# A hybrid decoder block: the attention stretch in source order on every engine, and a PSUM bank of its own for the scans' unused operand

## The chip, the cores and the metric

The kernel runs on one core of a Trainium2 chip. The core has TensorE (PE in the profile; its weight loads are PEld), VectorE (DVE), ScalarE (ACT), GpSimd (POOL) and SyncE (SP), which issues the transfers. The metric is the device time of one execution in microseconds (us), the median of the runs shown.

## The reference

One decoder layer over 2048 tokens of 1024 columns. Three token mixers run on one normalised input projection, their outputs are normalised per head, joined, projected by `w_out` and added to the input; a SwiGLU feed-forward follows. The change touches the stretch in which the mixers run. The attention there is stick-breaking attention with 6 heads of 64 columns:

```python
z = einsum('bhqd,bhkd->bhqk', q, k) * d ** -0.5         # strictly causal
A[t, s] = sigmoid(z[t, s]) * prod_{s < j < t} (1 - sigmoid(z[t, j]))
out = A @ v
```

The other two mixers (4 heads each) are gated linear recurrences over the tokens:

```python
S_t = diag(f_t) S_{t-1} + k_t^T v_t ;  o_t = q_t S_t
```

## The kernel before, in words

The program is traced from top to bottom; a planner then orders the instructions of each engine. It keeps data dependences, prefers what stands earlier in the source, and puts a later instruction ahead where its own costs say that an earlier one isn't ready. The order so made is fixed: at run time each engine works through its list and waits where an operand isn't there.

Three phases follow one another: the input projections (to about 753 us), the attention stretch (753 to about 1615 us), and the output projection's rest with the feed-forward.

**The attention stretch.** It is cut into 240 slots (line 1301 and the loop after it). A unit is one head, one group of 512 queries and one block of 512 keys; each unit has four slots, one for 128 queries each. In a slot `n` the source calls, in this order:

- `z_step(n)`: TensorE writes the scores `z` into one of two PSUM banks (pool `f_pz`). ScalarE makes `kp = sigmoid(-z)` (L994) and a second sigmoid of `z` (L997), which goes into the SBUF tile `w`, or back into `z` for those slots whose weights VectorE multiplies (`on_dve`: slot 0 of a unit, or slots 0 and 2 in the first query group; 66 of 240). VectorE's scan (L998) makes the running products `pr` out of `kp`; its second tensor operand takes no part in the result (`op1=ALU.bypass`) and is a broadcast column of `z`. Then `w = w * pr` (or `z * pr`) on VectorE (L1002) or on GpSimd (L1004). There are two `kp` tiles, two `pr` tiles and 7 `w` buffers.
- half of the slot's share of recurrence steps (`rec_step`). Such a step has TensorE write chunk scores `sch` or `scg` into a bank of the pool `c_pss` (three banks), VectorE read them out under a mask (L1082, `st_h`, `st_g`) and multiply the queries by decays (L1078, L1119), and GpSimd multiply keys and decays (L1113, L1124, L1128). Outputs, transposed keys and updates of the state go through the same three banks.
- `t_step(n - 5)`: TensorE transposes four 128-column pieces of `w` into `wt` (L107), ScalarE copies them to `wth` (L1014, 8 buffers).
- the rest of the recurrence steps, or, when the recurrences are done, one step of the output projection (`out_.steps()`: the products `po`, norms on VectorE, L830 to L862).
- `a_step(n - 7)`: TensorE multiplies `wth` with the values.

TensorE's instructions of this stretch go through the class `Chain`, which ties each to the one before it without a semaphore, so that TensorE runs them in source order:

```python
for n in (self.last, self.after):
    if n is not None:
        tc.add_manual_dep(i, n, NOSYNC, reason="order")
```

The other engines' orders are the planner's. The transfers of SyncE are the planner's too, and the change doesn't touch that.

Of the kernel before, what the change touches and what calls it, by code (L numbers as in the profile page):

```python
# [8 lines left out]
F32 = mybir.dt.float32  # L9
# [4 lines left out]
AF = mybir.ActivationFunctionType  # L14
ALU = mybir.AluOpType
AX = mybir.AxisListType
PSUM = bass.MemoryType.PSUM
DRAM = bass.MemoryType.DRAM

P = 128  # L20
# [7 lines left out]
LAG_T = 5  # L28
# [34 lines left out]
def hybrid_block(ctx: ExitStack, tc: tile.TileContext, x, norm_mix_g, w_in, gla_w_decay,  # L63
# [2 lines left out]
    nc = tc.nc  # L66
    x, out = x[0], out[0]
    w_in, w_out, w_up, w_dn = w_in[0], w_out[0], w_ffn_up[0], w_ffn_down[0]
    act, dve, pool, pe, dma = nc.scalar, nc.vector, nc.gpsimd, nc.tensor, nc.sync


    def rsqrt_newton(small, v, n, tag):
# [19 lines left out]
    class Chain:  # L92
# [13 lines left out]
        def transpose(self, *a, **k):  # L106
            self._add(nc.tensor.transpose(*a, **k))  # L107

    tpe = [pe]
    NOSYNC = mybir.DependencyInfo(mybir.DependencyClass.NoSync,  # L110
                                  mybir.DependencyReason.SCHED_ONLY)

    def mm3(ps, pairs, n_lo=None):

        n = len(pairs)
# [8 lines left out]
    def open_pool(stack, name, bufs, space=None, side=None):  # L124
        kw = {} if space is None else {"space": space}
        if side is not None:
            kw["side"] = side
        return stack.enter_context(tc.tile_pool(name=name, bufs=bufs, reuse_waits="tile", **kw))
# [206 lines left out]
    class Stage:  # L335


        def __init__(self, p, stg, xtp, half):
            self.p, self.half, self.xtp = p, half, xtp
            self.b = [stg.tile([P, KH, 512], F32, tag=f"sg{j}", name=f"stg{p}_{j}")  # L340
                      for j in range(4)]
            self.xs = {}
# [585 lines left out]
    with ExitStack() as ph:  # L928
# [8 lines left out]
        prc = ExitStack()  # L937
        rio = open_pool(prc, "c_io", NB)
        rec = open_pool(prc, "c_rec", 2)
        ps_s = open_pool(prc, "c_pss", 3, PSUM)  # L940
        ps_o = ps_s
        tpe[0] = ch

# [10 lines left out]
        for g in G_ORDER:  # L954
            for h in range(0, SH, 2):
                for c in range(g, -1, -1):
                    for j in range(2):
                        u = Unit()
                        u.h, u.g, u.c, u.diag, u.i, u.j = h + j, g, c, c == g, len(units), j
                        units.append(u)  # L960

        def z_step(u, b):
            h, g, c = u.h, u.g, u.c
            if b == 0:
                if u.diag:
                    u.q = sio.tile([P, 2, 512], F32, tag="sq", name=f"sq{h}_{g}", bufs=3)
                    for s in range(2):
                        dma.dma_start(u.q[64 * s:64 * s + 64],
                                      sq_s[h // 2][g][:, 64 * (h % 2):64 * (h % 2) + 64, :]
                                      .rearrange("j p t -> p j t"))  # L970
                    u.carry = [1.0] * 4
                else:
                    p = units[u.i - 2]
                    u.q, u.carry = p.q, p.last
                u.last = []
                k = sio.tile([P, 512], F32, tag="sk", name=f"sk{h}_{g}_{c}")
                dma.dma_start(k, sk_s[h][c].rearrange("j p t -> (j p) t"))
                if u.j == 0:
                    u.v = sio.tile([P, 4, P], F32, tag="sv", name=f"sv{h}_{g}_{c}")
                    dma.dma_start(u.v, sv_s[c][:, h * SD:(h + 2) * SD]  # L980
                                  .rearrange("(n p) d -> p n d", p=P))
                u.k, u.ws = k.bitcast(F32R), []
            n = (b + 1) * P if u.diag else 512
            q = u.q.bitcast(F32R)[:, :, b * P:(b + 1) * P]
            z = ps_z.tile([P, 512], F32, tag="z", name=f"z{h}_{g}_{c}_{b}")[:, :n]
            ch.matmul(z, q[:, 0], u.k[:, :n], start=True, stop=False)
            ch.matmul(z, q[:, 1], u.k[:, :n], start=False, stop=not u.diag)
            if u.diag:
                ch.matmul(z[:, b * P:], identb, negm, start=False, stop=True)
            kp = kps[b % NKP][:, 512 - n:]  # L990
            w = sbw.tile([P, 512], F32, tag="w", name=f"w{h}_{g}_{c}_{b}", bufs=7)[:, :n]
            at = 4 * (g - c) + 2 * u.j + b // 2
            pr = prs[b % 2][:, at:at + 513]
            act.activation(kp[:, :n], z, AF.Sigmoid, scale=-1.0)  # L994
            kr = kp[:, n::-1] if n < 512 else kp[:, ::-1]
            on_dve = b in DVE_B0 if g == 0 else b == DVE_B
            act.activation(z if on_dve else w, z, AF.Sigmoid)  # L997
            dve.tensor_tensor_scan(pr[:, n::-1], kr, z[:, 0:1].to_broadcast([P, n + 1]),  # L998
                                   u.carry[b], op0=ALU.mult, op1=ALU.bypass)
            u.last.append(pr[:, 0:1])  # L1000
            if on_dve:
                dve.tensor_tensor(w, z, pr[:, 1:n + 1], op=ALU.mult)  # L1002
            else:
                pool.tensor_tensor(w, w, pr[:, 1:n + 1], op=ALU.mult)  # L1004
            u.ws.append(w)

        def t_step(u, s):
            t0 = s * P if u.diag else 0
            nm = f"{u.h}_{u.g}_{u.c}_{s}"
            wt = ps_w.tile([P, 512], F32, tag="wt", name="wt" + nm)  # L1010
            for b in range(t0 // P, 4):
                ch.transpose(wt[:, b * P:(b + 1) * P], u.ws[b][:, s * P:(s + 1) * P], ident)
            wh = sbw.tile([P, 512], F32, tag="wth", name="wth" + nm, bufs=8)[:, t0:]
            act.activation(wh, wt[:, t0:], AF.Copy)  # L1014
            u.wt = getattr(u, "wt", []) + [(wh, t0)]

# [275 lines left out]
        def rec_step(part):  # L1292
            nonlocal ns
            while ns < REC_STEPS * ((done + part) / total) ** REC_POW:
                ns += 1
                if next(step, 0) == 0:
                    return 1
            return 0

        outs = None  # L1300
        for n in range(n_slot + LAG_A):
            d = 0.0
            if n < n_slot:
                z_step(units[n // 4], n % 4)
                d = (n % 4 + 1) / 16 if units[n // 4].diag else 0.25
            if outs is None and rec_step(d / 2):
                for _ in wo_step:
                    pass
                prc.close()
                out_.open()  # L1310
                outs = out_.steps()
            if 0 <= n - LAG_T < n_slot:
                t_step(units[(n - LAG_T) // 4], (n - LAG_T) % 4)
            if outs is None:
                rec_step(d)
            else:
                for _ in range(OUT_RATE):
                    out_done = next(outs)
            done += d
            if folds:  # L1320
                o_step(*folds.pop())
            if 0 <= n - LAG_A < n_slot:
                a_step(units[(n - LAG_A) // 4], (n - LAG_A) % 4)
            if n >= WO_SLOT and n % 4 == 0:
                next(wo_step, None)
        o_step(*folds.pop())
# [289 lines left out]
```

## Time and profile before

| | |
|---|---|
| time, median of 3 runs | 3163.24 us (3161.28 to 3166.27) |
| profiled execution | 3166.77 us, span 3164.4 us |
| mean granted TensorE clock | 0.947 of full speed |
| PE busy over the span | 2836.1 us (90%) |
| DVE | 2115.8 us (67%) |
| ACT | 1282.6 us (41%) |
| POOL | 1423.3 us (45%) |

The first scan of line 998 starts at 754.9 us and the last at 1601.0 us; the last recurrence product of line 1078 starts at 1405.0 us. A busy time is the sum of an engine's instruction times; a wait is idle time of an engine, put down to what released it. An engine whose share is high in a stretch can still be waiting for another in that stretch, so the waits are read next to the shares.

### The profile page before, as it was taken

How to read it: one execution, taken by the hardware profiler on the slowest of the kernel's cores; microseconds unless marked ns; L12 is line 12 of the kernel's file. 1: busy time of each engine (PE TensorE's matmuls, PEld its weight loads, DVE VectorE, ACT ScalarE, POOL GpSimd, SP SyncE). 2: the span in 40 equal slices, each digit the busy share in tenths (PEclk: the TensorE clock that was granted, in tenths of full speed). 3: DMA queues.
4: the chain of work that ended last, by engine and by line, in shares of the span. 5: the costliest groups of instructions: out<-in, count | busy, mean ns of one | idle time of the engine just before them, and what ended most of it. 6: DMA issues, size and time to landing. Idle time of an engine off the chain costs nothing.

```text
span 3164.4 us, 43263 instructions
## 1 busy us (share of the span) xinstructions
PE 2836.1 (90%) x14882; PEld 2321.6 (73%) x14882; DVE 2115.8 (67%) x3808; ACT 1282.6 (41%) x2386; POOL 1423.3 (45%) x1402
## 2 busy tenths in 40 slices
PE   5898999997888888888788799999999998999887
PEld 5887878987666666665556578888788887777766
DVE  8886665876778777888867565555755553574453
ACT  5554534453555554554532243333433332322222
POOL 5342444344655555542221244444544443566244
PEclk8999999998989988998988899999999999999998
DMA  3534442436533322223345442222422224832474
GB/s 121 154 106 139 133 137 94 128 94 170 164 104 99 93 82 80 76 96 95 101 144 190 139 137 89 81 80 80 147 80 85 87 89 163 325 120 80 136 259 150
DMA packets 346091, 389.78 MB, mean 123 GB/s; under 512 B 59152, under 2 KB 258064, under 8 KB 344080
## 3 DMA queue, kind: packets, MB, share of 16 engines
q1 hardware_dynamic: 341776, 381.77, 38.1%
q0 software_dynamic: 4096, 5.25, 0.5%
q8 instruction: 118, 1.93, 0.3%
q14 instruction: 101, 0.83, 0.1%
HBM read 278.93 MB, written 108.00 MB: 122 GB/s over the span
## 4 chain that ended last, share of the span: by engine, by line
PE 56%; DVE 16%; DMA 5%; issue 5%; POOL 2%; ACT 2%; SPq 1%; DVEq 0%; POOLq 0%; ACTq 0%
PE gu L1404 9%; PE gu L1405 9%; PE gu L1403 8%; PE dn L1569 4%; DVE pr L998 4%; PE dn L1570 4%; PE dn L1571 3%; PE z L104 3%; PE av L104 2%; PE sch L104 2%; PE wt L107 2%; DVE m L840 1%; PE po L104 1%; PE scg L104 1%; DVE hq L1078 1%
## 5 line engine op out<-in xcount | busy, mean ns | idle before, releaser
L1404 PE MATMUL gu<-al,uh 128*128 128x512 f32 x1232 | 482.7, 392 | 7.0 <-DVE al L249 6.8
L1403 PE MATMUL gu<-ah,uh 128*128 128x512 f32 x1232 | 481.7, 391 | 5.0 <-ACT ah L248 4.9
L1405 PE MATMUL gu<-ah,ul 128*128 128x512 f32 x1232 | 481.0, 390 | 0.0
L249 POOL TENSOR_TENSOR ul<-bs,uh 128x512 fp32r<-128x512 f32 x176 | 241.3, 1372 | 240.8 <-ACT uh L248 236.5
L1004 POOL TENSOR_TENSOR w<-w,pr 128x512 f32<-128x512 f32 (+1 forms) x174 | 194.6, 1119 | 279.3 <-DVE pr L998 208.5
L1569 PE MATMUL dn<-dbh,dah 128*128 128x512 f32 x616 | 232.5, 407 | 52.3 <-ACT dbh L248 38.9
L1404 PEld LDWEIGHTS gu<-al,uh 128*128 128x128 f32 x1232 | 232.2, 188 | 61.5 <-DVE al L249 13.5
L249 POOL TENSOR_TENSOR ul<-us,uh 128x512 fp32r<-128x512 f32 x132 | 177.1, 1342 | 214.3 <-ACT uh L248 214.3
L1403 PEld LDWEIGHTS gu<-ah,uh 128*128 128x128 f32 x1232 | 232.5, 189 | 55.2 <-ACT ah L248 7.1
L1405 PEld LDWEIGHTS gu<-ah,ul 128*128 128x128 f32 x1232 | 232.3, 189 | 47.8
L245 DVE TENSOR_TENSOR h<-h,gu 128x512 f32<-128x512 f32 x176 | 120.9, 687 | 204.9 <-PE gu L1405 123.0
L104 PE MATMUL z<-sk,sq 128*128 128x512 f32 (+1 forms) x480 | 175.8, 451 | 86.8 <-DVE pr L998 46.0
L1570 PE MATMUL dn<-dbl,dah 128*128 128x512 f32 x616 | 242.9, 397 | 7.9 <-POOL dbl L249 7.8
L1571 PE MATMUL dn<-dbh,dal 128*128 128x512 f32 x616 | 240.0, 394 | 0.0
L248 ACT ACTIVATE uh<-bs 128x512 fp32r<-128x512 f32 x176 | 111.3, 634 | 305.1 <-PE gu L1404 300.8
L994 ACT ACTIVATE kp<-z 128x512 f32<-128x512 f32 (+1 forms) x240 | 128.1, 534 | 258.7 <-PE z L104 233.7
L104 PEld LDWEIGHTS z<-sk,sq 128*128 128x128 f32 x480 | 82.6, 213 | 180.5 <-DVE pr L998 73.3
L998 DVE TENSOR_TENSOR_SCAN pr<-kp,pr,z 128x513 f32<-128x513 f32 x144 | 182.1, 1271 | 20.4 <-ACT w L997 12.6
L1569 PEld LDWEIGHTS dn<-dbh,dah 128*128 128x128 f32 x616 | 120.5, 196 | 80.8 <-ACT dbh L248 40.5
L107 PE MATMUL wt<-ident,w 128*128 128x128 f32 x816 | 150.1, 300 | 19.4 <-POOL w L1004 19.0
L248 ACT ACTIVATE uh<-us 128x512 fp32r<-128x512 f32 x132 | 83.4, 633 | 191.5 <-PE gu L1404 126.3
L249 DVE TENSOR_TENSOR dal<-ar,dah 128x1024 fp32r<-128x1024 f32 x44 | 65.5, 1492 | 127.4 <-ACT dah L248 127.4
(379 smaller groups left out, 7556.8 us busy)
## 6 DMA issues: line engine op xcount, KB each, us to landing
us<-in_w_ffn_up SPq DMA_DIRECT2D x88, 512.0 KB, 3.8
ar<-hs_s SPq DMA_DIRECT2D x88, 512.0 KB, 4.2
hs_s<-h SPq DMA_DIRECT2D x44, 512.0 KB, 2.6
br<-in_w_ffn_down SPq DMA_DIRECT2D x88, 256.0 KB, 4.1
sk<-sk_s SPq DMA_DIRECT2D x60, 256.0 KB, 2.9
st<-xs_s SPq DMA_DIRECT2D x14, 1024.0 KB, 5.5
xt<-in_x SPq DMA_DIRECT2D x24, 512.0 KB, 4.9
sq<-sq_s SPq DMA_DIRECT2D x48, 256.0 KB, 4.7
```

The lines of the kernel that those rows point to most:

```text
L104: self._add(nc.tensor.matmul(*a, **k))
L107: self._add(nc.tensor.transpose(*a, **k))
L248: act.activation(wh, st, AF.Copy)
L249: eng.tensor_tensor(wl, st, wh.bitcast(F32), op=ALU.subtract)
L998: dve.tensor_tensor_scan(pr[:, n::-1], kr, z[:, 0:1].to_broadcast([P, n + 1]), u.carry[b], op0=ALU.mult, op1=ALU.bypass)
L1004: pool.tensor_tensor(w, w, pr[:, 1:n + 1], op=ALU.mult)
L1403: pe.matmul(pv, bh[:, k, :], ah[:, :, k, :], start=(k == 0), stop=False)
L1404: pe.matmul(pv, bh[:, k, :], al[:, :, k, :], start=False, stop=False)
L1405: pe.matmul(pv, bl[:, k, :], ah[:, :, k, :], start=False, stop=(k == KH - 1))
L1569: pe.matmul(pss[i], ah[:, ts_], bh, start=(k == 0), stop=False)
L1570: pe.matmul(pss[i], ah[:, ts_], bl, start=False, stop=False)
L1571: pe.matmul(pss[i], al[:, ts_], bh, start=False, stop=(k == NK - 1))
```

## The change: what it does

- A class `Seq` wraps ScalarE, VectorE and GpSimd. While `Seq.on` is set, each instruction issued through it is tied to the one before it on its engine, without a semaphore, as `Chain` does for TensorE. It is set in the slots' loop, but for the output projection's steps, the loads of `w_out` and the switch from the recurrences to the output projection.
- In a slot, `t_step(n - 5)` now stands ahead of `z_step(n)`.
- GpSimd's `w * pr` is put on a list (`late`) and issued at the head of the next slot, behind GpSimd's work of its own slot.
- The second sigmoid always writes `w` in SBUF, and VectorE's product reads `w` there too.
- The scan's unused operand is a column of ones in a PSUM bank of its own (`c_ps1`); when the recurrences' pools are closed, that bank goes with them, and the operand is then `kr`, the scan's own first operand, in SBUF.
- The banks of `c_pss` go from three to two; the `w` buffers from 7 to 8, the `wth` buffers from 8 to 7.

```diff
--- before.py
+++ after.py
@@ -66,7 +66,29 @@
     nc = tc.nc
     x, out = x[0], out[0]
     w_in, w_out, w_up, w_dn = w_in[0], w_out[0], w_ffn_up[0], w_ffn_down[0]
-    act, dve, pool, pe, dma = nc.scalar, nc.vector, nc.gpsimd, nc.tensor, nc.sync
+    NOSYNC = mybir.DependencyInfo(mybir.DependencyClass.NoSync,
+                                  mybir.DependencyReason.SCHED_ONLY)
+
+    class Seq:
+
+        on = False
+
+        def __init__(self, eng):
+            self.eng, self.last = eng, None
+
+        def __getattr__(self, op):
+            def issue(*a, **k):
+                r = getattr(self.eng, op)(*a, **k)
+                if Seq.on:
+                    i = getattr(r, "ins", r)
+                    if self.last is not None:
+                        tc.add_manual_dep(i, self.last, NOSYNC, reason="order")
+                    self.last = i.name
+                return r
+            return issue
+
+    act, dve, pool = Seq(nc.scalar), Seq(nc.vector), Seq(nc.gpsimd)
+    pe, dma = nc.tensor, nc.sync
 
 
     def rsqrt_newton(small, v, n, tag):
@@ -107,9 +129,6 @@
             self._add(nc.tensor.transpose(*a, **k))
 
     tpe = [pe]
-    NOSYNC = mybir.DependencyInfo(mybir.DependencyClass.NoSync,
-                                  mybir.DependencyReason.SCHED_ONLY)
-
     def mm3(ps, pairs, n_lo=None):
 
         n = len(pairs)
@@ -937,7 +956,10 @@
         prc = ExitStack()
         rio = open_pool(prc, "c_io", NB)
         rec = open_pool(prc, "c_rec", 2)
-        ps_s = open_pool(prc, "c_pss", 3, PSUM)
+        ps_s = open_pool(prc, "c_pss", 2, PSUM)
+        ps_1 = open_pool(prc, "c_ps1", 1, PSUM)
+        ones = [ps_1.tile([P, 512], F32, name="one")[:, 0:1]]
+        dve.memset(ones[0], 1.0)
         ps_o = ps_s
         tpe[0] = ch
 
@@ -958,6 +980,8 @@
                         u = Unit()
                         u.h, u.g, u.c, u.diag, u.i, u.j = h + j, g, c, c == g, len(units), j
                         units.append(u)
+
+        late = []
 
         def z_step(u, b):
             h, g, c = u.h, u.g, u.c
@@ -988,20 +1012,20 @@
             if u.diag:
                 ch.matmul(z[:, b * P:], identb, negm, start=False, stop=True)
             kp = kps[b % NKP][:, 512 - n:]
-            w = sbw.tile([P, 512], F32, tag="w", name=f"w{h}_{g}_{c}_{b}", bufs=7)[:, :n]
+            w = sbw.tile([P, 512], F32, tag="w", name=f"w{h}_{g}_{c}_{b}", bufs=8)[:, :n]
             at = 4 * (g - c) + 2 * u.j + b // 2
             pr = prs[b % 2][:, at:at + 513]
             act.activation(kp[:, :n], z, AF.Sigmoid, scale=-1.0)
             kr = kp[:, n::-1] if n < 512 else kp[:, ::-1]
-            on_dve = b in DVE_B0 if g == 0 else b == DVE_B
-            act.activation(z if on_dve else w, z, AF.Sigmoid)
-            dve.tensor_tensor_scan(pr[:, n::-1], kr, z[:, 0:1].to_broadcast([P, n + 1]),
+            act.activation(w, z, AF.Sigmoid)
+            dve.tensor_tensor_scan(pr[:, n::-1], kr,
+                                   ones[0].to_broadcast([P, n + 1]) if ones else kr,
                                    u.carry[b], op0=ALU.mult, op1=ALU.bypass)
             u.last.append(pr[:, 0:1])
-            if on_dve:
-                dve.tensor_tensor(w, z, pr[:, 1:n + 1], op=ALU.mult)
+            if b in DVE_B0 if g == 0 else b == DVE_B:
+                dve.tensor_tensor(w, w, pr[:, 1:n + 1], op=ALU.mult)
             else:
-                pool.tensor_tensor(w, w, pr[:, 1:n + 1], op=ALU.mult)
+                late.append(lambda: pool.tensor_tensor(w, w, pr[:, 1:n + 1], op=ALU.mult))
             u.ws.append(w)
 
         def t_step(u, s):
@@ -1010,7 +1034,7 @@
             wt = ps_w.tile([P, 512], F32, tag="wt", name="wt" + nm)
             for b in range(t0 // P, 4):
                 ch.transpose(wt[:, b * P:(b + 1) * P], u.ws[b][:, s * P:(s + 1) * P], ident)
-            wh = sbw.tile([P, 512], F32, tag="wth", name="wth" + nm, bufs=8)[:, t0:]
+            wh = sbw.tile([P, 512], F32, tag="wth", name="wth" + nm, bufs=7)[:, t0:]
             act.activation(wh, wt[:, t0:], AF.Copy)
             u.wt = getattr(u, "wt", []) + [(wh, t0)]
 
@@ -1300,27 +1324,36 @@
         outs = None
         for n in range(n_slot + LAG_A):
             d = 0.0
+            Seq.on = True
+            while late:
+                late.pop()()
+            if 0 <= n - LAG_T < n_slot:
+                t_step(units[(n - LAG_T) // 4], (n - LAG_T) % 4)
             if n < n_slot:
                 z_step(units[n // 4], n % 4)
                 d = (n % 4 + 1) / 16 if units[n // 4].diag else 0.25
             if outs is None and rec_step(d / 2):
+                Seq.on = False
                 for _ in wo_step:
                     pass
                 prc.close()
+                ones.clear()
                 out_.open()
                 outs = out_.steps()
-            if 0 <= n - LAG_T < n_slot:
-                t_step(units[(n - LAG_T) // 4], (n - LAG_T) % 4)
+                Seq.on = True
             if outs is None:
                 rec_step(d)
             else:
+                Seq.on = False
                 for _ in range(OUT_RATE):
                     out_done = next(outs)
+                Seq.on = True
             done += d
             if folds:
                 o_step(*folds.pop())
             if 0 <= n - LAG_A < n_slot:
                 a_step(units[(n - LAG_A) // 4], (n - LAG_A) % 4)
+            Seq.on = False
             if n >= WO_SLOT and n % 4 == 0:
                 next(wo_step, None)
         o_step(*folds.pop())
```

## Rows read from the trace of the kernel before

**Rows 1.** Three stretches by time: busy us of each engine, granted clock.
```profile
core 0: us, PE busy (x) PEld busy (x) DVE busy (x) ACT busy (x) POOL busy (x), PEclk, DMA share, GB/s
753.00:1395.00 642.00, 550.65 (x3842) 420.63 (x3842) 498.80 (x894) 337.97 (x812) 361.73 (x594) 0.90 0.38 105
1395.00:1615.00 220.00, 177.54 (x873) 122.33 (x872) 173.00 (x452) 109.48 (x209) 58.83 (x53) 0.90 0.34 109
1355.00:1455.00 100.00, 80.37 (x505) 56.54 (x504) 87.57 (x213) 54.43 (x113) 36.96 (x43) 0.90 0.30 100
```

**Rows 2.** Waits of TensorE's matmuls, 753 to 1615 us.
```profile
engine line waited for: us in total, times, longest us
PE z L104 <- DVE pr L998: 46.0, 25, 5.3
PE z L104 <- DVE w L1002: 22.2, 17, 3.0
PE wt L107 <- POOL w L1004: 19.0, 15, 3.7
PE z L104 <- DVE ms L833: 12.8, 3, 7.0
```

**Rows 3.** Timeline, one stall: start us, us, instruction, [idle before <-releaser].
```profile
1120.45 0.73 PE L104 MATMUL z<-sk,sq 128*128 128x512 f32 x2
...
1123.35 0.60 ACT L997 ACTIVATE w<-z 128x512 f32<-128x512 f32 x1 [1.01 <-PE wt L107]
...
1125.72 0.69 DVE L1082 COPY_PREDICATED st_h<-masks,sch 128x256 f32<-128x256 int8 x1
1126.21 1.25 DVE L998 TENSOR_TENSOR_SCAN pr<-kp,pr,z 128x513 f32<-128x513 f32 x1
...
1127.51 1.22 PE L104 MATMUL z<-sk,sq 128*128 128x512 f32 x2 [3.41 <-DVE pr L998]
...
1129.36 0.68 DVE L1002 TENSOR_TENSOR w<-z,pr 128x512 f32<-128x512 f32 x1
```

**Rows 4.** Waits of VectorE, 753 to 1615 us.
```profile
DVE st_h L1082 <- PE sch L104: 41.5, 32, 4.8
DVE pr L998 <- ACT z L997: 41.2, 19, 6.4
DVE pr L998 <- ACT w L997: 26.7, 21, 4.1
DVE qx_g L1078 <- PE scg L104: 20.3, 12, 4.0
DVE st_g L1082 <- PE scg L104: 15.4, 19, 1.8
```

**Rows 5.** Instructions on tile z: count, ns min/median/max, first and last start.
```profile
L998 DVE TENSOR_TENSOR_SCAN pr<-kp,pr,z x144: 1241/1272/1285, 855.3 to 1601.0; 128x513 f32<-128x513 f32 x144
...
L1002 DVE TENSOR_TENSOR w<-z,pr x66: 259/662/693, 755.3 to 1586.9; 128x512 f32<-128x512 f32 x36, 128x128 f32<-128x128 f32 x24, 128x384 f32<-128x384 f32 x6
```

**Rows 6.** Line 1078, a product of two SBUF tensors: ns min/median/max.
```profile
L1078 DVE TENSOR_TENSOR hq<-hq,th x96: 386/616/1501, 763.6 to 1400.3; 128x256 f32<-128x256 f32 x96
```

**Rows 7.** Line 1119, the same at 512 columns.
```profile
L1119 DVE TENSOR_TENSOR hq<-hq,hf x16: 722/1020/1543, 758.8 to 1365.8; 128x512 f32<-128x512 f32 x16
```

**Rows 8.** Timeline, GpSimd's product beside VectorE's.
```profile
1106.10 1.09 POOL L1004 TENSOR_TENSOR w<-w,pr 128x512 f32<-128x512 f32 x1 [0.99 <-DVE pr L998]
1106.26 1.22 DVE L1078 TENSOR_TENSOR hq<-hq,th 128x256 f32<-128x256 f32 x1
```

**Rows 9.** Line 1082, masked reads of the scores: count, ns min/median/max.
```profile
L1082 DVE COPY_PREDICATED st_h<-masks,sch x96: 395/570/781, 758.2 to 1393.5; 128x256 f32<-128x256 int8 x96
L1082 DVE COPY_PREDICATED st_g<-masks,scg x96: 398/570/786, 760.7 to 1398.4; 128x256 f32<-128x256 int8 x96
```

**Rows 10.** Line 998's scans, 1395 to 1615 us: busy us (count).
```profile
1395.00:1615.00 220.00, 62.01 (x52) 0.90 0.34 109
```

**Rows 11.** GpSimd by line, 1395 to 1615 us: busy us, mean ns | idle.
```profile
L1004 POOL TENSOR_TENSOR w<-w,pr 128x512 f32<-128x512 f32 x35 | 42.5, 1214 | 133.2 <-DVE pr L998 70.6 <-DVE ms L833 21.0 <-PE wt L107 12.3
```

## The prediction

> **What bounds the kernel now.** I read the busy shares by time first, because the change touches only the attention stretch. I cut that stretch at 1395 us, about where the recurrences end and the output projection takes their place in the slots. In the first part TensorE is busy for 550.65 of 642 us (86%) and VectorE for 498.80 (78%); in the second 177.54 of 220 (81%) and 173.00 (79%) [rows 1]. No engine is full, and the clock granted to TensorE is 0.90 in both. So two engines near their limits keep holding each other up, and the next view is who waits for whom.
>
> TensorE's longest waits are for a free bank of z: 46.0 us until a scan had ended, 22.2 until VectorE's product on z, 12.8 behind norm work that VectorE did first; 81.0 us together. Another 19.0 us are transposes that wait for GpSimd's product [rows 2]. VectorE waits too: 77.2 us for scores (41.5 + 20.3 + 15.4), and 67.9 us for ScalarE's second sigmoid in front of a scan (41.2 + 26.7), although the scan's result doesn't use it [rows 4].
>
> The timeline of one stall shows how both hang together [rows 3]. The second sigmoid at 1123.35 waited 1.01 us for transposes to free one of the seven w buffers. VectorE's list then has a masked read between the scans, the scan ends at 1127.46, and only then does the z product start, 3.41 us late. The product on z at 1129.36 holds its bank past the scan. After the idle time the two z matmuls take 1.22 us where a pair at 1120.45 took 0.73: TensorE's clock had fallen towards its lower level (1.2 of 2.4 GHz). A stall thus costs more than its length.
>
> **The change part by part.**
>
> *The bank of z.* The scan and VectorE's product no longer read z. A bank is then free when the second sigmoid has ended, which needs the first one, which needs its kp tile, which the scan two slots before must have left. TensorE gains about two slots of room, and the reason for the 81.0 us [rows 2] is gone. The scan no longer waits for the second sigmoid either (67.9 us [rows 4], part of which is only the same lateness of z seen from VectorE). With eight w buffers and the transposes ahead, the sigmoid's wait of 1.01 us in rows 3 has no place any more.
>
> *What VectorE pays.* Its scan keeps its price: 1241 to 1285 ns for 513 columns in all 144 runs, and the product with z in PSUM stays between 259 and 693 ns over its 66 [rows 5]. Products of two SBUF tensors don't: 386 to 1501 ns (median 616) at 256 columns [rows 6], 722 to 1543 (median 1020) at 512 [rows 7]. The row beside it says why: GpSimd's product starts at 1106.10 and lasts 1.09 us, VectorE's starts at 1106.26 and lasts 1.22, so it ended 0.29 us after GpSimd's, near the time that it needs alone [rows 8]. After the change the 66 products have both operands in SBUF. I take the median's excess over the minimum, 0.30 us, for each (the rows of 512 columns are the same shape as most of them): 20 us, spread as the scans are, of which 52 of 240 come after 1395 us [rows 10]: 16 and 4 us. Bounds: nothing, and 66 x 0.82 = 54 us (the maximum's excess).
>
> The 52 scans after 1395 us take kr as second operand and so become instructions with two SBUF operands as well. GpSimd is busy for 58.83 of these 220 us, 27% [rows 1], mostly with products of 1.21 us [rows 11]. A scan that starts at any time meets one in 27% of cases and waits half of it: 0.27 x 0.61 x 52 = 8 us. Bounds: nothing, and a whole product each, 52 x 1.21 = 63 us. On this the Trainium skill speaks against the change: SBUF — State Buffer, Who interferes with whom, says that "A DVE instruction with two SBUF inputs contends with a GpSimd instruction that reads SBUF", and that the later one waits for the whole of the other. Rows 8 agree with it; that a scan obeys it no run here shows yet.
>
> *The order.* ScalarE is at 338 of 642 us [rows 1], so its fixed order hides in its idle time; without that cover kp(n) would come one copy later in each slot. GpSimd's product now stands behind the key products of its own slot. In source order they would wait behind it for the scan; here it waits for them. The transposes ask for it two slots after its z, so a delay is hidden unless GpSimd falls behind; it is at 361.73 of 642. If it does, the 19.0 us of rows 2 grow, and z(n), now behind the transposes, is late with them; I put this at 0 to 19 us more and take none. The transposes issue no transfer, and SyncE's list is not tied; I cost that at nothing.
>
> *VectorE's order* is the largest unknown. Scans, masked reads and query products now come strictly as TensorE makes them. A masked read whose scores are late holds the scan behind it, and the other way round.
>
> *Two score banks.* TensorE may write a third set of scores only when VectorE has read the first. There are 192 masked reads of 0.57 us [rows 9]. Between a set and the one after next lies about a slot of TensorE work, so I take no wait. Bounds: nothing, and a whole read each, 192 x 0.57 = 109 us.
>
> **The sum.** With the bank of z gone from between them, the engine with the most unavoidable work per slot and the least slack is VectorE: 498.80 + 16 = 514.8 us in the first part, 173.00 + 4 + 8 = 185 in the second. What share can it reach? 78% and 79% now; 87.57 of 100 us in the best stretch of the trace, 1355 to 1455 [rows 1]. I take 85%, nearer that row than the present, because its two large waits lose their cause, and below it, since strict order and two banks bring some back. 514.8 / 0.85 = 605.6 (36.4 less), 185 / 0.85 = 217.6 (2.4 less): 38.8 us less. TensorE would then be at 550.65 / 605.6 = 91% with the present clock; fewer stalls should raise the clock and lower this.
>
> The profiled execution took 3166.77 us (span 3164.4, 2.4 around it), 0.1% above the median of 3163.24. I take the difference from the median: 3163.2 - 38.8 = **3124 us**. Bounds of the share: no better than now (0.777 and 0.786) gives 662.5 + 235.3 us, 36 more, 3199. At 0.93 it is 553.5 + 198.9, 110 less, 3054; the first of these is already at TensorE's busy time, so more needs a higher clock.
>
> **The rivals.**
>
> *A larger gain* (75 to 130 us less, 3033 to 3088, at its middle 3063). The whole 81 us go, and the clock rises. At 0.90 mean, a fifth of 862 us lies at the lower level (172 us); if a quarter of it is won back, 43 us of TensorE work halve, some 20 us. For it speaks how closely rows 3 tie slow matmuls to the stall; against it that VectorE must then run at 92% or so.
>
> *No change* (3157 to 3170). VectorE sets the pace anyway, and TensorE waits at the next place that depends on it, the score banks and transposes, for as long as it waited at z. For it: both engines are within 8 points of each other in rows 1. Against it: VectorE itself waited for TensorE and ScalarE, 145 us in rows 4.
>
> *Slower by the two banks.* In strict order a masked read stands behind a scan that waits for kp; TensorE waits for that read before its next scores, and z of the next slot is late. The 81 us are lost again when each of the 192 reads holds TensorE for 0.42 us; at 0.57 it is 109 - 81 = 28 us more, 3191. For it: VectorE waited 77.2 us for scores, so it runs close behind TensorE, with little lead to spend. Against it: in rows 2 no such wait is among the large ones with three banks.
>
> *Slower by the shared read path of VectorE and GpSimd.* GpSimd's product is released by the end of one scan, and may always be under way when the next SBUF operand is wanted. With a whole product for each late scan the second part is (173 + 4 + 63) / 0.85 = 282 us, 62 more, and the total 26 more: 3189. It decides from 0.78 us a scan. By the Trainium skill's rule cited above (SBUF — State Buffer, Who interferes with whom) a scan pays this whenever the two meet; the trace agrees for products [rows 8], and how often a scan would meet one it can't say.
>
> That the change doesn't do what it says I give nothing of its own: the order is forced by the ties, and the scan loses z by its operand.
>
> **How the numbers follow.** Chances: the forecast (10 to 75 us less) 0.52, the larger gain 0.15, no change 0.11, the banks 0.12, the read path 0.10. A measurement here tells about 0.2%, 6.3 us, from nothing. Faster by more: 0.52 + 0.15 and a little of no change, 0.69; within: 0.10; slower: 0.21. The range runs from 3055, where the larger gain meets the bound at 93%, to 3185, which takes in no change and the milder half of the slower cases; the forecast alone spans 3088 to 3153.
>
> **What would show it.** Right: z no longer waits for a scan or a product; the scan no longer waits for the second sigmoid; VectorE's share in the first part is 83 to 88%; the granted clock of the stretch is above 0.90; the products of line 1002 have a median near 0.95 us at 512 columns, and late scans reach beyond 1.29 us. Wrong: new waits of sch or scg for VectorE's masked reads of 40 us or more; transposes that wait for GpSimd for more than 40 us; late scans of 2 us as a rule; or a VectorE that waits for scores for longer than the 77.2 us of now.

## The result and the profile after

The changed kernel took 3183.41 us (median of 5 runs, 3182.78 to 3196.44) against 3165.7 for the kernel before in the same runs: ratio 1.0065, 95% interval 1.0041 to 1.0088. It is slower by 0.65% (18 us between the medians); the prediction was 39 us faster.

The stretches first, as in [rows 1] (us, busy us of each engine with its instructions, granted clock, DMA share). The recurrences' last output starts at 1447.7 us here and at 1407.2 before, so the cut is at 1448. The first two rows are the changed kernel, the last two the kernel before, cut at the end of its own recurrences:

```profile
753.00:1448.00 695.00, 565.11 (x3941) 431.81 (x3942) 514.43 (x912) 343.64 (x829) 362.82 (x602) 0.89 0.35 98
1448.00:1640.00 192.00, 163.26 (x792) 109.72 (x791) 169.09 (x433) 102.75 (x194) 57.77 (x44) 0.92 0.39 125
...
753.00:1407.00 654.00, 560.83 (x3939) 428.70 (x3939) 508.11 (x911) 344.48 (x827) 367.13 (x601) 0.90 0.37 104
1407.00:1597.00 190.00, 153.07 (x710) 103.83 (x709) 152.18 (x391) 97.36 (x185) 52.16 (x44) 0.89 0.36 116
```

The two parts went opposite ways. The part with the recurrences got 40 us longer (the end of the recurrences moved from 1407.2 to 1447.7; both attention stretches start within 1 us of 754). The part after it got shorter: its 48 slots run from 1448 to 1622, 174 us, where before 48 slots ran from 1407 to 1597, 190 us. VectorE's work in the first part is 514.43 us; over 695 us that is 74%, not 85%. It lies near the forecast's 514.8 only because the cut is later: in the same part before it was 508.11, so 6 us were added where the forecast has 16.

TensorE's waits, to be read against [rows 2]:

```profile
PE sch L126 <- DVE hq L81: 57.8, 22, 4.8
PE wt L129 <- POOL w L81: 17.6, 16, 2.0
PE scg L126 <- DVE qx_g L81: 12.0, 7, 6.3
...
PE sch L126 <- DVE st_h L81: 7.6, 8, 2.6
```

and VectorE's, against [rows 4] (instructions issued through `Seq` all carry its line, 81):

```profile
DVE pr L81 <- ACT kp L81: 138.5, 105, 7.7
DVE st_h L81 <- PE sch L126: 37.7, 24, 3.0
DVE qx_g L81 <- PE scg L126: 3.3, 5, 1.6
```

Every wait of z for VectorE is gone: of the 81.0 us nothing is left. In their place TensorE waits 57.8 us for the recurrences' query products, which doesn't stand among [rows 2] (5.7 us before). VectorE's scan waits 138.5 us for kp, where it waited 67.9 us for the second sigmoid.

Where the 57.8 us come from is seen by asking for the matmuls that wait. 54.2 of them lie ahead of 16 groups of one form, `sch` of 128 columns, once in each of the 16 chunks of the second mixer, 3.4 us each (the sum of the idle times in the timeline's rows of this form; before, the same 16 waited 1.3 us together). One of them on the timeline:

```profile
1124.76 0.60 ACT L81 ACTIVATE kp<-z 128x512 f32<-128x512 f32 x1
...
1125.25 0.59 ACT L81 ACTIVATE w<-z 128x512 f32<-128x512 f32 x1
1125.45 1.22 DVE L81 TENSOR_TENSOR_SCAN pr<-kp,one 128x513 f32<-128x513 f32 x1 [1.18 <-ACT kp L81]
1125.73 0.70 ACT L81 ACTIVATE hq<-hq 128x64 f32<-128x64 f32 x4
1126.59 1.12 DVE L81 TENSOR_TENSOR hq<-hq,hf 128x512 f32<-128x512 f32 x2
...
1127.86 1.15 PE L126 MATMUL sch<-hq,hk 128*128 128x128 f32 x8 [3.14 <-DVE hq L81]
```

These are the scores of the second and third level of a chunk, taken in one pass. Ahead of them ScalarE copies part of the queries aside (`hold`, four copies) and VectorE multiplies the queries by the decays, twice. In the source this is all one step: where `hold` is used, these two lines don't end the step between the products and the scores.

```python
if not (h == 1 and hold is not None):
    yield 1
```

In the planned order the copies and the products ran ahead of their place. In the kernel before, for the ninth chunk, the copies ran 66 us ahead of the products, and these ended 9 us ahead of the scores, which didn't wait:

```profile
1015.10 0.71 ACT L1171 ACTIVATE hq<-hq 128x64 f32<-128x64 f32 x4 [0.77 <-DMA hq<-hq_s]
...
1082.25 0.90 DVE L1119 TENSOR_TENSOR hq<-hq,hf 128x512 f32<-128x512 f32 x1
1083.18 0.43 DVE L1078 TENSOR_TENSOR hq<-hq,hf 128x256 f32<-128x256 f32 x1
...
1092.91 1.13 PE L104 MATMUL sch<-hq,hk 128*128 128x128 f32 x8
```

In source order they can't: the copies stand behind the slot's two sigmoids, the products behind the slot's scan, and TensorE, which is in source order too, has nothing else that it may start. After 11 of the 16 waits the matmuls then run slower as well: one took 2.04 us where the one above took 1.15.

```profile
1043.77 2.04 PE L126 MATMUL sch<-hq,hk 128*128 128x128 f32 x8 [4.11 <-DVE hq L81]
```

### The profile page after: what moved, and what is told of

Same layout as the page of the kernel before. It is cut to its first block, busy times and chain, and to the rows that moved or that the text cites. A ratio compares the mean times of both kernels' runs of the same rounds, so it can differ in the third digit from the quotient of the medians.

```text
span 3181.4 us, 43565 instructions
## 1 busy us (share of the span) xinstructions
PE 2826.1 (89%) x14882; PEld 2313.5 (73%) x14882; DVE 2128.2 (67%) x3809; ACT 1278.5 (40%) x2386; POOL 1425.1 (45%) x1402
## 3 DMA queue, kind: packets, MB, share of 16 engines
q8 instruction: 119, 1.95, 0.3%
## 4 chain that ended last, share of the span: by engine, by line
PE 49%; DVE 11%; issue 4%; DMA 3%; ACT 2%; POOL 2%; SPq 0%; DVEq 0%; ACTq 0%; POOLq 0%
PE gu L1437 9%; PE gu L1438 9%; PE gu L1436 8%; PE dn L1602 3%; PE dn L1603 3%; PE dn L1604 3%; PE av L126 2%; PE wt L129 2%; DVE pr L81 2%; PE sch L126 2%; PE z L126 2%; DVE m L81 1%; PE scg L126 1%; DMA m<-mx_s 1%; DVE acc L81 1%
## 5 line engine op out<-in xcount | busy, mean ns | idle before, releaser
L81 ACT ACTIVATE wth<-wt 128x512 f32<-128x512 f32 x240 | 128.1, 534 | 257.9 <-PE wt L129 256.9
L126 PE MATMUL sch<-hq,hk 128*128 128x64 f32 (+3 forms) x1024 | 121.8, 272 | 80.7 <-DVE hq L81 57.8
L129 PEld LDWEIGHTS wt<-ident,w 128*128 128x128 f32 x816 | 101.6, 154 | 116.8 <-issue 56.8
L126 PEld LDWEIGHTS sch<-hq,hk 128*128 128x128 f32 (+2 forms) x1024 | 110.4, 185 | 96.6 <-issue 73.4
L81 DVE TENSOR_TENSOR_SCAN pr<-kp,pr,one 128x513 f32<-128x513 f32 x105 | 133.9, 1275 | 57.8 <-ACT kp L81 57.6
```

What stands on the lines that cost most here:

```text
L81: r = getattr(self.eng, op)(*a, **k)
L126: self._add(nc.tensor.matmul(*a, **k))
```

## The experiments

All ratios are to the kernel before, run on the same chip in the same job, with the 95% interval. "The 16 waits" is the sum of TensorE's idle time ahead of the 16 groups named above, from the timeline of each run.

**VectorE left to the planner.**

```diff
-    act, dve, pool = Seq(nc.scalar), Seq(nc.vector), Seq(nc.gpsimd)
+    act, dve, pool = Seq(nc.scalar), nc.vector, Seq(nc.gpsimd)
```

> The changed kernel with VectorE left to the planner; ScalarE and GpSimd stay in source order, operands and banks as changed. Theory A (VectorE's strict order costs: its scan waits for kp at the head of the list while query products that TensorE wants stand behind it): the recurrence part (753 us to the last output of the recurrences, 654 us before, 695 after) falls to 650 us or less, the scan's wait for kp (138.5 us after) to under 60 and the wait of sch for the query products (57.8 us) to under 25; 3125 to 3155 us. Theory B (two score banks instead of three): no better than after, 3175 to 3190. Theory C (contention of VectorE's SBUF products with GpSimd's): 3175 to 3190 too.

3168.98 us, ratio 0.9996 (0.998 to 1.0013). By the ratios some 20 us better than the changed kernel, but not what theory A asks: the scan's wait for kp fell to 76.7 us, and the wait of `sch` for the query products stayed, at 61.3 (the 16 waits: 56.3). So the loss doesn't need VectorE to be tied.

**The order alone**, with the operands and banks of before. The other parts of the order stay as changed: the transposes first, GpSimd's late products, the 8 and 7 buffers.

```diff
-            act.activation(w, z, AF.Sigmoid)
-            dve.tensor_tensor_scan(pr[:, n::-1], kr,
-                                   ones[0].to_broadcast([P, n + 1]) if ones else kr,
+            on_dve = b in DVE_B0 if g == 0 else b == DVE_B
+            act.activation(z if on_dve else w, z, AF.Sigmoid)
+            dve.tensor_tensor_scan(pr[:, n::-1], kr, z[:, 0:1].to_broadcast([P, n + 1]),
...
-        ps_s = open_pool(prc, "c_pss", 2, PSUM)
+        ps_s = open_pool(prc, "c_pss", 3, PSUM)
```

> Source order on all engines, with the operands and the banks of before: the scan reads z, VectorE's products read z, three score banks. Theory A: the recurrence part stays at 685 us or more and the time at 3180 to 3215, since z is held by the scan again. Theories B and C: the part is back at 655 us or less, 3140 to 3168.

3181.82 us, ratio 1.0037 (1.002 to 1.0054). Slower without any change of operands or banks: the 16 waits are 63.7 us. Theories B and C fall as the cause of the loss. Its stretches, with the recurrences' end at 1447, and its waits of z for another engine:

```profile
753.00:1447.00 694.00, 558.02 (x3940) 429.86 (x3941) 520.40 (x912) 342.71 (x829) 356.74 (x607) 0.88 0.36 99
1447.00:1620.00 173.00, 146.70 (x709) 98.89 (x708) 151.89 (x393) 97.46 (x185) 51.70 (x43) 0.92 0.41 129
...
PE z L126 <- DVE w L81: 11.5, 8, 3.6
```

So in source order z hardly waited for VectorE even while the scan still read it: 11.5 us are left of 81.0. Both parts are as long as in the changed kernel (694 and 173 us against 695 and 174), and the intervals of the two ratios overlap. In source order the new operands and banks gained nothing that can be measured.

**The operands and banks alone**, in the planner's order: the kernel before with the second sigmoid always into `w`, the column of ones in its own bank, two score banks, and `kr` after the recurrences.

```diff
-            act.activation(z if on_dve else w, z, AF.Sigmoid)
-            dve.tensor_tensor_scan(pr[:, n::-1], kr, z[:, 0:1].to_broadcast([P, n + 1]),
+            act.activation(w, z, AF.Sigmoid)
+            dve.tensor_tensor_scan(pr[:, n::-1], kr,
+                                   ones[0].to_broadcast([P, n + 1]) if ones else kr,
...
-        ps_s = open_pool(prc, "c_pss", 3, PSUM)
+        ps_s = open_pool(prc, "c_pss", 2, PSUM)
+        ps_1 = open_pool(prc, "c_ps1", 1, PSUM)
```

> The planner's order of before, with the changed operands and banks: second sigmoid into w, a column of ones in its own bank, two score banks, the scan on kr after the recurrences. Theory A: z no longer waits for scans (46.0 us before) or products (22.2), and the order costs nothing: 3120 to 3152 us. Theory B: new waits of sch and scg for the masked reads of 40 us or more, 3172 to 3195. Theory C: VectorE's busy time in the stretch up by 30 us or more, 3170 to 3190.

3126.43 us, ratio 0.9855 (0.9821 to 0.989): 1.45% faster, and so a version that beats both kernels. Its stretches, with the recurrences' end at 1380:

```profile
753.00:1380.00 627.00, 551.24 (x3944) 417.11 (x3944) 516.78 (x912) 345.38 (x829) 373.96 (x602) 0.93 0.39 109
1380.00:1560.00 180.00, 148.21 (x721) 99.39 (x719) 160.18 (x403) 98.60 (x187) 57.11 (x45) 0.93 0.40 126
```

and its largest waits of TensorE over both:

```profile
PE wt L107 <- POOL w L1007: 13.9, 13, 5.4
PE mt L107 <- DVE m L840: 9.3, 1, 9.3
PE z L104 <- ACT w L999: 9.0, 11, 3.6
```

The bank of z is now waited for through the second sigmoid, 9.0 us where VectorE cost 81.0 before, VectorE's share of the first part is 82% and of the second 89%, and the clock is 0.93 instead of 0.90. The 16 waits are 0.8 us.

**Three score banks** in the changed kernel, with `kr` as the operand throughout, since no bank is left for the ones.

```diff
-        ps_s = open_pool(prc, "c_pss", 2, PSUM)
-        ps_1 = open_pool(prc, "c_ps1", 1, PSUM)
-        ones = [ps_1.tile([P, 512], F32, name="one")[:, 0:1]]
-        dve.memset(ones[0], 1.0)
+        ps_s = open_pool(prc, "c_pss", 3, PSUM)
+        ones = []
```

> The changed kernel with three score banks again; there is no bank left for the ones, so the scan's unused operand is kr in SBUF throughout. Theory A: the waits of scores for banks go (16 us of them after), the scan's wait for kp stays over 100 us; within 10 us of the changed kernel, 3173 to 3195. Theory B: the recurrence part falls by 30 us or more, 3140 to 3160. Theory C: scans over 1.3 us become common (some 190 of them in the recurrence part, at 0.2 to 0.5 us each on VectorE) and it is slower than the changed kernel by 20 us or more.

3202.68 us, ratio 1.0092 (1.0058 to 1.0125). It is not faster, and the 16 waits are 64.4 us. The run changes two things, the banks and the scans' operand, and doesn't price either alone; that the two banks are not what costs is shown by the order alone, which has three banks and is slow all the same.

The 16 waits, which all kernels tied so far share and the planned one doesn't have, made the theory of the hold step (H in what follows).

**The hold step ended before its scores**, all else as changed.

```diff
-                if not (h == 1 and hold is not None):
-                    yield 1
+                yield 1
...
-REC_STEPS = 425
+REC_STEPS = 445
```

> The changed kernel, source order everywhere; in a recurrence chunk of the second mixer the copies and products of the held queries end a step of their own, where before the next scores followed in the same step (16 steps more, so the number of steps planned over the slots goes from 425 to 445, which keeps the recurrences' end at about the same slot). Theory H (the loss is 16 waits of some 3.4 us, 54.2 us in all in the changed kernel, in which TensorE's next scores wait in the same step for four copies on ScalarE and two products on VectorE that strict order no longer lets run ahead): these waits fall under 12 us and the time to 3115 to 3145 us. Theory A (VectorE's scan at the head of its list waiting for kp sets the pace): that wait stays over 100 us and the time at 3170 or more.

3143.23 us, ratio 0.9899 (0.9872 to 0.9926). The 16 waits fell from 54.2 to 9.3 us, 45 less, and the ratio from 1.0065 to 0.9899, some 50 us. VectorE's scan waits for kp as long as ever:

```profile
DVE pr L81 <- ACT kp L81: 134.3, 105, 6.1
```

So that wait, VectorE's largest in this stretch, is not what cost these 50 us, and theory A falls as their cause. The run also paces the recurrences by 445 steps in place of 425; their end stays at the same place among the slots, within one. The run with only the hold step untied, below, does without this.

**Transposes first**, with the 8 and 7 buffers, on top of operands alone in the planner's order.

```diff
+            if 0 <= n - LAG_T < n_slot:
+                t_step(units[(n - LAG_T) // 4], (n - LAG_T) % 4)
             if n < n_slot:
                 z_step(units[n // 4], n % 4)
...
-            if 0 <= n - LAG_T < n_slot:
-                t_step(units[(n - LAG_T) // 4], (n - LAG_T) % 4)
```

> Operands alone as in the third run above, the planner's order, and the transposes ahead of the scores in each slot with 8 w and 7 wth buffers. Theory H: none of the 16 waits comes back, 3105 to 3140 us. Rival T (the transposes' place, with z behind them, is what costs): 3150 us or more, with waits of wt for GpSimd's product above 30 us.

3133.44 us, ratio 0.9876 (0.9858 to 0.9895); the 16 waits 0.3 us. The transposes' wait for GpSimd grew from 13.9 to 24.8 us, and the intervals of this run and of operands alone overlap. Their place isn't the cause in the planner's order. This kernel is the base of the next three.

**One engine tied at a time**, on top of it: ScalarE, VectorE, GpSimd (the last with its products one slot late, as in the change).

```diff
-    act, dve, pool, pe, dma = nc.scalar, nc.vector, nc.gpsimd, nc.tensor, nc.sync
...
+    act, dve, pool = Seq(nc.scalar), nc.vector, nc.gpsimd
...
```

> The kernel with transposes first, and ScalarE alone in source order; VectorE and GpSimd are the planner's. Theory H: the four copies of the held queries stand behind the slot's sigmoids, so the 16 waits are back at 35 to 60 us and the time is 25 to 50 us above the kernel with transposes first. Theory A: nothing changes by more than 8 us, since VectorE is free.

> The kernel with transposes first, and VectorE alone in source order. Theory H: the two products behind the copies stand behind the slot's scan, so part of the 16 waits is back, 20 to 50 us, and the time 15 to 45 us above the kernel with transposes first. Theory A: the scan's wait for kp is over 100 us and the time 40 us or more above, whatever the 16 waits are.

> The kernel with transposes first, and GpSimd alone in source order, its weight products issued one slot late. Theory H: the held queries' copies and products are free, so the 16 waits stay under 10 us, and the time stays within 15 us of the kernel with transposes first (3133). Theory A (any strict order costs its part): 20 us or more above it, as ScalarE alone (44) and VectorE alone (66) did.

| tied | us | ratio (95%) | the 16 waits, us |
|---|---|---|---|
| none | 3133.44 | 0.9876 (0.9858 to 0.9895) | 0.3 |
| ScalarE | 3177.23 | 1.0012 (0.9998 to 1.0027) | 63.6 |
| VectorE | 3199.86 | 1.0077 (1.0053 to 1.0101) | 63.0 |
| GpSimd | 3121.7 | 0.9861 (0.9837 to 0.9886) | 0.3 |

Either of the two engines that take part in the hold step brings the waits back when tied, and GpSimd, which has no part in it, costs nothing that can be measured. With ScalarE tied, TensorE's largest wait is the same one:

```profile
PE sch L126 <- DVE hq L1102: 57.2, 17, 4.5
```

With VectorE tied, ScalarE is free to make its copies early, and did: for the ninth chunk 84 us ahead of the products. These still waited for their place, behind a scan that itself stood 1.84 us waiting for kp:

```profile
1037.10 0.71 ACT L1195 ACTIVATE hq<-hq 128x64 f32<-128x64 f32 x4 [0.39 <-DMA hq<-hq_s]
...
1120.63 1.22 DVE L81 TENSOR_TENSOR_SCAN pr<-kp,one 128x513 f32<-128x513 f32 x1 [1.84 <-ACT kp L1018]
1121.77 2.07 DVE L81 TENSOR_TENSOR hq<-hq,hf 128x512 f32<-128x512 f32 x2
...
1123.99 2.04 PE L126 MATMUL sch<-hq,hk 128*128 128x128 f32 x8 [4.75 <-DVE hq L81]
```

VectorE tied costs 20 us more than ScalarE tied with the same 16 waits (its scan waits 127.4 us for kp, against 66.9), so its order has a further price there; what it consists of these runs don't show. Its 66 us above the base lie beyond what theory H gave this run and meet what theory A gave it, so H alone doesn't account for VectorE's order.

**Only the hold step untied**, in the changed kernel.

```diff
+                    on, Seq.on = Seq.on, False
                     held = hold(up)
+                    Seq.on = on
...
                 if h == 1:
+                    on = Seq.on
+                    if hold is not None:
+                        Seq.on = False
...
                     q_mul(1, tcur)
+                    Seq.on = on
```

> The changed kernel in which only the instructions of the 16 hold steps are not tied: the four copies on ScalarE and the products with the decay that follow on VectorE. All else is in source order. Theory H (strict order costs because these few can't run ahead): the 16 waits fall under 15 us and the time to 3120 to 3150 us, as with a step of their own (3143). Theory A (strict order as such costs, and the step of their own helped by spreading the work): 3165 us or more.

3143.53 us, ratio 0.9931 (0.9908 to 0.9953). The 16 waits are 1.2 us. With nothing else changed, the copies for the ninth chunk now run 70 us ahead of the products, and these end 7 us ahead of the scores, which don't wait:

```profile
1016.98 0.72 ACT L81 ACTIVATE hq<-hq 128x64 f32<-128x64 f32 x4 [0.27 <-DMA hq<-hq_s]
...
1087.47 2.04 DVE L81 TENSOR_TENSOR hq<-hq,hf 128x512 f32<-128x512 f32 x2
...
1096.87 1.13 PE L126 MATMUL sch<-hq,hk 128*128 128x128 f32 x8
```

This is the narrowest test: a few instructions a chunk decide the sign of the change. It stays above the untied base (0.9876; the intervals don't meet), so the order costs some 0.5% besides, for a reason that these runs don't show.

**The hold step ended early in the planned order**, on top of operands alone (the same edit as above).

> Operands alone (3126 us) with the hold step's products in a step of their own, the planner's order. Theory H: the planner had hidden these waits already (0.8 us left of 54), so nothing to gain, 3115 to 3138 us. Rival: the step helps by itself wherever it is, 3085 to 3105.

3122.31 us, ratio 0.986 (0.9834 to 0.9887), the same as without it: the planner had hidden that wait. The step of its own isn't a gain by itself.

**Three score banks in the planned order**, `kr` throughout, on top of operands alone.

> Operands alone in the planner's order, but three score banks and kr in SBUF as the scan's unused operand throughout. If the two banks cost (5 to 15 us of waits for masked reads are left in the run with operands alone) and SBUF operands are cheap: 3105 to 3120 us. If the scan meets GpSimd's products in the recurrence part as it does after it (39 scans 0.15 us longer each): 193 scans of it, 29 us of VectorE, and 3135 to 3160.

3134.32 us, ratio 0.9898 (0.9869 to 0.9927). It is no faster, and the scans show the price of their second SBUF operand: the 144 long ones with a carry take 1416 ns in the mean, against 1272 for the 105 that operands alone runs with the ones in PSUM.

```profile
L998 DVE TENSOR_TENSOR_SCAN pr<-kp,pr 128x513 f32<-128x513 f32 x144 | 203.7, 1416 | 11.4 <-ACT kp L995 10.3 <-POOL w L1005 0.9
```

All scans together are 294.3 us here and 267.5 with operands alone, 27 more (29 were foreseen), for some 8 us between the medians (14 by the ratios, whose intervals overlap).

## Why the prediction failed, step by step

**The bank of z: right in the planner's order.** With operands alone the time is 3126.43 us, 2 us from the 3124 predicted for the whole change. The 81.0 us of waits for VectorE are gone, with 9.0 for the second sigmoid in their place; the clock of the stretch rose from 0.90 to 0.93, VectorE's share rose to 82% and 89%; the one share taken for both, 85%, lies between them. That the total fits so well is partly luck: the sum takes 36.4 us from the first part and 2.4 from the second, and the run gained 27 and 17. The second part is short in the changed kernel too: 174 us for its 48 slots, 172 with operands alone, 190 before. But the order alone has 173, so either change shortens it, and they don't add up.

**The order: wrong, and this is the step that failed.** The prediction set ScalarE's fixed order at nothing: it "hides in its idle time", for it is busy for half of the stretch. VectorE's order it called the largest unknown, and gave it no price but a share of 85% in place of 87. Tied alone, ScalarE costs 44 us (3177 against 3133), and VectorE 66 (3200). ScalarE's idle time in sum doesn't matter where four copies must be done between two neighbouring instructions of TensorE, and the fixed order puts two sigmoids ahead of them. I named what a late score would do to a scan, but didn't follow the recurrence's steps for one in which a product and the scores that read it stand in the same step. The source lines show it: in every other step a `yield` lies between them. Before, TensorE was already in source order and only the planner's freedom on ScalarE and VectorE covered this place; the change takes away that cover. The 16 waits grew by 53 us (54.2 against 1.3); between operands alone and the changed kernel lie 57 us of the medians (2.1% by the ratios). Untying only the hold step brings back 1.3 of these 2.1%, ending it early 1.7.

The sum also added the parts up: the gain of the operands, less a share that the order brings back. They don't add. The operands are worth 1.45% in the planner's order and nothing in source order, where z waited for VectorE for 11.5 us already. Seen the other way, the order costs 0.4% with the old operands and 2.1% with the new ones.

**What VectorE pays: right in kind, too large in size.** The mean over the 36 products of 512 columns and over the 39 late scans with a carry in the changed kernel:

```profile
L81 DVE TENSOR_TENSOR_SCAN pr<-kp,pr 128x513 f32<-128x513 f32 x39 | 53.7, 1379 | 3.2 <-ACT kp L81 1.9 <-POOL w L81 0.9
...
L81 DVE TENSOR_TENSOR w<-w,pr 128x512 f32<-128x512 f32 x36 | 25.4, 704 | 3.6
```

The products of all widths went from 34.7 to 38.2 us, 3.5 more where 20 were taken; at 512 columns a median near 0.95 us was expected, and the mean is 0.70. In the planner's order they cost more, 46.5 us with operands alone. The late scans are 1379 ns where they were 1274, 4 us for the 47 that take `kr`, where 8 us for 52 were taken. A scan with two SBUF operands does meet GpSimd's products, then, as the cited sentence of the Trainium skill has it (SBUF — State Buffer, Who interferes with whom): the longest took 2.10 us where none before passed 1.285. Five of the 39 took 2.02 to 2.10 us, each begun at most 0.34 us after a product of GpSimd; no other took more than 1.29. One of the five:

```profile
1501.85 1.27 POOL L81 TENSOR_TENSOR w<-w,pr 128x512 f32<-128x512 f32 x1 [7.34 <-DVE pr L81]
...
1502.18 2.03 DVE L81 TENSOR_TENSOR_SCAN pr<-kp,pr 128x513 f32<-128x513 f32 x1
```

How seldom they meet kept this rival from deciding.

**Two score banks: right.** The waits of scores for masked reads (`sch` for `st_h` and `st_g`) are 7.6 and 3.2 us in the changed kernel, far from the 81 at which the rival would have won. The two runs with three banks and `kr` throughout were no faster, though each of them also pays for the scans' second SBUF operand.

**The rivals.** The outcome has the sign of the two slower rivals and the cause of neither. None of the four signs of being wrong that the prediction lists came true; the VectorE that waits for scores for longer than 77.2 us, for one, waited 41. The wait sat on TensorE, for the query products, and I had listed only masked reads among the ways it could wait for VectorE. The rival of no change, by which TensorE "waits at the next place that depends on it", was nearest, but the new place has nothing to do with z.

**What stays open.** The changed kernel with the hold step untied or ended early (0.9931, 0.9899) stays behind the untied base (0.9876); the interval of the first lies apart from the base's, that of the second overlaps it. The scan's wait for kp, 113.5 and 134.3 us in these, is not shown to be the reason. What is left with the hold step untied, some 17 us, is near the 20 us by which VectorE tied costs more than ScalarE tied, and near what the changed kernel gains with VectorE left to the planner; that the three are one thing is not shown. VectorE tied alone has a longer median than all three engines tied (3199.86 against 3183.41), but the intervals of their ratios overlap, so no difference is shown. Whether the operands would gain anything in source order once the hold step is untied was not run, and which part of the order alone shortens the second part wasn't either.

## What to carry to other kernels

Before an order is forced on an engine, go through the source for the places where an instruction and its consumer on another engine stand next to each other with nothing in between; here each of the 16 paid 2.7 to 4.8 us, with only one of the two other engines tied as with both, and the idle shares didn't show it. Change operands and order in separate runs, and don't add up what they give: here the operands gave 1.45% in the one order and nothing in the other. And the largest wait of a profile need not set the time: 134 us of waiting for kp stayed while the kernel became 1.7% faster.

## What was not expected of the hardware

That a stall costs more than its length the prediction had taken from [rows 3]; how uneven this is was not expected. Of the 16 groups of score matmuls, 11 took 1.9 to 2.05 us after their wait, five 1.14 or 1.15. The granted clock over the two groups shown above, the one that took 2.04 us and the one that took 1.15:

```profile
1043.70:1045.90 2.20, 2.13 (x10) 2.16 (x11) 0.05 (x1) 0.00 (x0) 0.00 (x0) 0.52 0.32 92
1127.80:1129.10 1.30, 1.24 (x11) 1.27 (x12) 0.05 (x1) 0.00 (x0) 0.00 (x0) 1.00 0.00 0
```

In the kernel before, where these groups hardly wait, three of them took 1.8 to 1.95 us and the others 1.07 to 1.15. Together they took 28.0 us against 20.1, so the 16 waits cost some 8 us in these matmuls alone, beside their own 54. The mean granted clock of the recurrence part was 0.89 with the 16 waits and 0.93 with operands alone.
